# The first two modulation sections with the weights as the stationary operand, and one context load instead of two

## The chip, the cores and the metric

The kernel runs on one core of a Trainium2 chip. The metric is the device time of one execution in microseconds, and shorter is better. The core has four engines that matter here: TensorE (PE, matmuls; its loads of the stationary operand are listed as PEld), VectorE (DVE), ScalarE (ACT) and GpSimd (POOL). SyncE (SP) only issues DMAs; ACT issues some as well. TensorE's clock has two levels, 1.2 and 2.4 GHz; a granted clock of 0.50 is the lower one and 1.00 the upper one.

## The reference

The reference is a two-layer backbone for 256 context tokens and 256 latent tokens of width 1024. Before anything else of a layer is computed, two conditioning vectors become six shifts, scales and gates each:

```python
cond_lat = jax.nn.silu(c)          # (1, 1024)
cond_ctx = jax.nn.silu(c_ctx)      # (1024,)
for layer in range(DEPTH):
    l_sh1, l_sc1, l_g1, l_sh2, l_sc2, l_g2 = jnp.split((cond_lat @ mod_w[layer] + mod_b[layer])[:, None, :], 6, axis=-1)
    c_sh1, c_sc1, c_g1, c_sh2, c_sc2, c_g2 = jnp.split(cond_ctx @ mod_w[layer] + mod_b[layer], 6, axis=-1)
    hl = modulate(rmsnorm(x, norm_g[layer, 0]), l_sh1, l_sc1)
    hc = modulate(rmsnorm(ctx, norm_g[layer, 0]), c_sh1, c_sc1)
    ...
```

`modulate(h, shift, scale)` is `h * (1 + scale) + shift`. All is float32. Sections 0 and 1 (the first shift and the first scale) of layer 0 are a product of a 2 x 1024 matrix with a 1024 x 2048 one, 8.4 MB of weights. The projections, the retention and attention of layer 0, its FFN, layer 1 and the experts follow, and each needs what came before it.

## The kernel before, in words

The program is written once in straight line, and the framework makes from it the order of instructions on each engine. That order is not wholly the written one: the second load of the context, written behind the mixer of layer 0 in `between`, is issued 23.93 us after the start. Each engine then works through its own order strictly in turn, and waits on semaphores. DMAs share a small set of semaphores, so that a queue can also wait for an older transfer that used the same one.

At the start, `columns` loads small vectors as rows, turns them with a TensorE transpose and copies the result into SBUF, so that element p of chunk k stands on partition p of column k (lines 198 to 211). It is used for `cvec` (the two conditioning vectors) and for `vec` (norm gains and other vectors; `voff` remembers where each begins). `cond` (line 216) holds the silu of both vectors, with k in columns and the two vectors in the first two of 32 lanes. `Xl` is the latent stream. The context is loaded into `Xc` by `load_xc`, first into `xnp0`, the pool of the start, and later again into `xcp`, a pool that stays.

`layer0` (line 492) calls `mod(0)`, then `first_two(xnp0)` and then `norm_hT(xnp0, range(4), A1, B1)`. In `first_two`, sixteen tiles `mraw` of 128 x 1024 weights (512 KB each, twelve buffers) come over SP's queue (line 300). Each serves two matmuls (line 313) in which `cond` (128 x 32) is the stationary operand and 512 weight columns stream through; the four blocks of 512 columns go to four groups of 32 output partitions. The result is a row vector: bias is added (line 315), four transposes turn it into columns (line 318), and `put` writes `B1` (line 290) and `A1 = (1 + scale) * gain` (line 288).

`norm_stats` (lines 376 to 387) takes the row statistics of all four token blocks and scales them into `xn`. `norm_hT` transposes `xn` (line 400), applies `A1` and `B1` (line 405, `htmp`) and splits the result into `hTh` and `hTl` (lines 272 and 273). The first projection starts at once behind it: `proj_tok` loads weights into `raw` (line 253), splits them into `whi` and `wlo` (lines 262 and 263) and multiplies in three passes (lines 267 to 269). Later sections of the modulation (`section`, lines 335 and 337) are done on VectorE, among the projections and the mixer.

Of the kernel before, what the change touches and what calls it, by code (L numbers as in the profile page):

```python
# [8 lines left out]
F32 = mybir.dt.float32  # L9
# [4 lines left out]
ALU = mybir.AluOpType  # L14
# [93 lines left out]
def seq(*gens):  # L108
    for g in gens:
        yield from g  # L110
# [20 lines left out]
def _build(top, tc, nc, V, S, G, T, I, O):  # L131
    cp = top.enter_context(tc.tile_pool(name="const", bufs=1))
    st = top.enter_context(tc.tile_pool(name="st", bufs=4))
    cur = {}

    def open_right(key, name, bufs=1):
        cur[key] = ExitStack()
        return cur[key].enter_context(tc.tile_pool(name=name, bufs=bufs, side="right", reuse_waits="tile"))
# [19 lines left out]
    def bank(kind):  # L158
        def take(name=kind):
            turn[kind] = turn.get(kind, -1) + 1  # L160
            n = use[kind][turn[kind] % len(use[kind])]
            return ps.tile([128, 512], F32, name=name, tag=f"b{n}")
        return take
    acc, tpp, att, ybank = (bank(k) for k in ("acc", "tp", "at", "y"))
# [4 lines left out]
    def const_(shape, name, dt=F32):  # L169
        return cp.tile(shape, dt, name=name)  # L170
# [11 lines left out]
    ident = cc("ident")  # L182
# [6 lines left out]
    xcp = open_right("xe", "xc")  # L189
# [5 lines left out]
    n0 = ExitStack()  # L195
    xnp0 = n0.enter_context(tc.tile_pool(name="n0", bufs=1))

    def columns(name, parts):

        n = sum(p[2] for p in parts)  # L200
        rows = xnp0.tile([n, 128], F32, name=name + "_r")
        r0 = 0
        for nm, src, k in parts:
            nc.scalar.dma_start(rows[r0:r0 + k], src)
            voff[nm] = r0
            r0 += k
        out = const_([128, n], name)
        t0 = tpp()
        T.transpose(t0[:, 0:n], rows, ident[0:n, 0:n])
        V.tensor_copy(out, t0[:, 0:n])  # L210
        return out

    voff = {}
    cvec = columns("cvec", (("c", I["c"].rearrange("o (k p) -> (o k) p", p=128), 8),
                            ("cc", I["c_ctx"].rearrange("(k p) -> k p", p=128), 8)))
    cond = const_([128, 8, 32], "cond")
# [3 lines left out]
    def load_xc(pool, src):  # L220
        cur["Xc"] = pool.tile([128, 2, D], F32, name="Xc")
        nc.scalar.dma_start(cur["Xc"], src.rearrange("(b p) d -> p b d", p=128))

    nc.scalar.dma_start(Xl, I["x"][0].rearrange("(b p) d -> p b d", p=128))
    load_xc(xnp0, I["ctx"][0])
    vec = columns("vec", (
        ("ng", I["norm_g"].rearrange("l i (k p) -> (l i k) p", p=128), 64),
        ("mu", I["rwkv_mu"].rearrange("o (k p) -> (o k) p", p=128), 15),
# [9 lines left out]
    def bcast_rows(dst, src, q=nc.scalar):  # L238
        n = src.shape[-1]
        q.dma_start(dst, bass.AP(tensor=src.tensor, offset=src.offset, ap=[[0, 128], [1, n]]))  # L240
# [36 lines left out]
    def mod(layer):  # L277
        A1, B1, A2, B2 = (const_([128, 8, 2], n) for n in ("A1", "B1", "A2", "B2"))

        by_half = lambda dst: dst.rearrange("p (s b) r -> p b s r", s=2)  # L280

        def put(q, tv):

            if q == 1:
                o = voff["ng"] + layer * 32
                ng = vec[:, o:o + 8].rearrange("p (s b) -> p b s", s=2)
                for r in range(2):
                    V.scalar_tensor_tensor(by_half(A1)[:, :, :, r], tv[:, :, :, r], 1.0, ng, op0=ALU.add, op1=ALU.mult)
            else:
                V.tensor_copy(by_half({0: B1, 3: B2, 4: A2}[q]), tv[:, :, :, 0:2])  # L290

        def bias(row, c0):
            G.memset(row, 0.0)
            n = row.shape[0]
            for r in range(2):
                nc.scalar.dma_start(row[r:n:32], I["mod_b"][layer, c0:c0 + 16 * n].rearrange("(s n) -> s n", s=n // 32))

        def load(pool, bufs, k, c0):
            w = pool.tile([128, 1024], F32, name="mraw", tag="mraw", bufs=bufs)
            nc.sync.dma_start(w, I["mod_w"][layer, k * 128:(k + 1) * 128, c0:c0 + 1024])  # L300
            return w

        def first_two(pool):

            row = cur["m"].tile([128, 1024], F32, name="modrow2", tag="part0", bufs=1)[:, :512]
            bias(row, 0)
            a = acc()
            for k in range(8):
                for s2 in range(2):
                    w = load(pool, 12, k, s2 * 1024)  # L310
                    for sj in range(2):
                        s = 2 * s2 + sj
                        T.matmul(a[32 * s:32 * s + 32], cond[:, k, :], w[:, sj * 512:(sj + 1) * 512],
                                 start=(k == 0), stop=(k == 7), tile_position=(0, 32 * s))
            V.tensor_tensor(row, row, a, op=ALU.add)
            t = tpp()
            for b in range(4):
                T.transpose(t[:, b * 128:(b + 1) * 128], row[:, b * 128:(b + 1) * 128], ident)
            tv = t.rearrange("p (b q s j) -> p q b s j", b=4, q=2, s=2)
            put(0, tv[:, 0])  # L320
            put(1, tv[:, 1])

        def section(q):

            w_ = cur["m"]
            streams = 1 if layer and q > 1 else 2
            part = [w_.tile([128, 1024], F32, name=f"part{r}", tag=f"part{r}", bufs=1) for r in range(streams)]
            for k in range(8):  # L330
                w = load(w_, 2, k, q * 1024)
                for r in range(streams):
                    c_ = cond[:, k, r:r + 1]
                    if k == 0:
                        V.tensor_scalar(part[r], w, c_, None, op0=ALU.mult)
                    else:
                        V.scalar_tensor_tensor(part[r], w, c_, part[r], op0=ALU.mult, op1=ALU.add)  # L337
                if k == 4:
                    rn = cur["h"].tile([128, 1024], F32, name="modrow", tag="raw", bufs=cur["rb"])
                    row, ngr = rn[0:64, 0:512], rn[0:64, 512:1024]  # L340
                    bias(row, q * 1024)
                    if q in (2, 4, 5):
                        G.memset(ngr, 1.0)
                        for r in range(2):
                            nc.scalar.dma_start(ngr[r:64:32], I["norm_g"][layer, {2: 1, 4: 2, 5: 3}[q]]
                                                .rearrange("(s n) -> s n", s=2))
                    if q == 4:
                        G.tensor_scalar(row, row, 1.0, None, op0=ALU.add)
                yield
            a = tpp()  # L350
            for r in range(streams):
                for s in range(2):
                    T.matmul(a[32 * s:32 * s + 32], cur["pick"][:, r], part[r][:, s * 512:(s + 1) * 512],
                             start=(r == 0), stop=(r == streams - 1), tile_position=(0, 32 * s))
            V.tensor_tensor(row, row, a[0:64], op=ALU.add)
            if q in (2, 4, 5):
                V.tensor_tensor(row, row, ngr, op=ALU.mult)
            if q > 1:
                for r in range(2):
                    nc.scalar.dma_start(I["mrow"][layer, q // 2 - 1, r, q % 2 * 1024:q % 2 * 1024 + 1024]  # L360
                                        .rearrange("(s n) -> s n", s=2), row[r:64:32])
            if q not in (2, 5):
                t = tpp()
                for b in range(4):
                    T.transpose(t[:, b * 64:(b + 1) * 64], row[:, b * 128:(b + 1) * 128], ident[0:64, 0:64])
                put(q, t[:, 0:256].rearrange("p (b s j) -> p b s j", b=4, s=2))

        def rowb(pool, n, r, name, tag=None, q=nc.scalar):

            t = pool.tile([128, D], F32, name=name, tag=tag or name, bufs=1)  # L370
            bcast_rows(t, I["mrow"][layer, n // 2 - 1, r, n % 2 * 1024:n % 2 * 1024 + 1024], q)
            return t

        mods[layer] = (first_two, section, rowb, A1, B1, A2, B2)

    def norm_stats(xnp, blks):
# [115 lines left out]
    def layer0():  # L492
        mod(0)
        first_two, section, rowb, A1, B1, A2, B2 = mods[0]
# [20 lines left out]
        de, xx, u, z, w, lg = (st.tile([128, 8], F32, name=f"lg_{i}", bufs=1) for i in range(6))  # L515
# [32 lines left out]
        t = {}  # L548
# [100 lines left out]
        m = seq(*(section(n) for n in (2, 3, 4)))  # L649
# [13 lines left out]
        first = {}  # L663

        def between():
            load_xc(xcp, I["ctx"][0])
            for i in range(4):
                first[i // 2, i % 2] = wsplit(gu_load(i // 2, i % 2, 0, 2), pre, G)

# [34 lines left out]
    def gu_load(k4, x, f0, n):  # L704
        w = (I["ffn_w_gate"], I["ffn_w_up"])[x][0]
        return wload(w[k4 * 512:(k4 + 1) * 512, f0 * 128:(f0 + n) * 128].rearrange("(a p) f -> p a f", p=128), 4, n * 128)
# [1176 lines left out]
```

## Time and profile before

| what | value |
|---|---|
| time, three runs | 2129.33, 2130.3, 2136.47 us, median 2130.3 |
| the profiled execution | 2132.66 us, of which 2130.9 us is the span from the first to the last instruction |
| TensorE busy | 2038.5 us (96%), mean granted clock 0.973 |
| VectorE busy | 1646.4 us (77%) |
| ScalarE busy | 1210.4 us (57%) |
| DMA | 494 MB, mean 232 GB/s |

The busy share is an average over stages that have different limits. For a change in the first 40 us, only that stage and what waits for it matter, and the busy share of TensorE is no measure of how fast its matmuls run.

### The profile page before, as it was taken

The page shows a single profiled execution, that of the slowest core. Times are in us where ns is not written, and L with a number is a line of the kernel's source. Part 1 is how long each engine was busy: PE and PEld are TensorE (multiplying, and loading weights), DVE is VectorE, ACT ScalarE, POOL GpSimd, SP SyncE. Part 2 cuts the span into 40 slices and gives each one's busy share as a digit, 9 for nine tenths or more (in the row PEclk, how much of TensorE's full clock was granted, in tenths as well). Part 3 has the DMA queues.
Part 4 walks back from the last instruction along what each step waited for, and adds up shares of the span by engine and source line. Part 5 has one row for each costly group of instructions (what it writes and reads, how often), then busy time and mean ns, then how long its engine had stood idle before and what let it go on. Part 6 is the DMA issues. An engine that isn't in the chain of part 4 may idle for free. (4 is left out here: it accounts for less than half of the span.)

```text
span 2130.9 us, 30220 instructions
## 1 busy us (share of the span) xinstructions
PE 2038.5 (96%) x11649; PEld 1621.1 (76%) x11650; DVE 1646.4 (77%) x2083; ACT 1210.4 (57%) x1557; POOL 152.6 (7%) x211
## 2 busy tenths in 40 slices
PE   7999989999999899869989999999999999999997
PEld 2767778878788666758877888888788787888875
DVE  3967793675556657687579999889989899889987
ACT  3543343222234445632348777777777777777775
POOL 0211110000000110184010000000000000000000
PEclk9999999999999999977899999999999999999999
DMA  8535352466645331100197999999999999999993
GB/s 299 163 106 169 105 175 60 149 229 206 190 157 188 102 90 55 34 19 12 62 333 267 361 307 362 337 352 360 349 347 341 352 376 353 334 356 361 360 352 143
DMA packets 224203, 494.00 MB, mean 232 GB/s; under 512 B 11355, under 2 KB 45262, under 8 KB 224054
## 3 DMA queue, kind: packets, MB, share of 16 engines
q1 hardware_dynamic: 219968, 482.62, 65.0%
q10 hardware_dynamic: 4086, 9.40, 1.3%
q8 instruction: 93, 1.52, 0.3%
q14 instruction: 56, 0.46, 0.1%
HBM read 490.87 MB, written 1.11 MB: 231 GB/s over the span
## 5 line engine op out<-in xcount | busy, mean ns | idle before, releaser
L273 DVE TENSOR_TENSOR mlo<-mraw,mhi 128x1024 fp32r<-128x1024 f32 x668 | 789.0, 1220 | 79.4 <-ACT mhi L272 62.6
L272 ACT ACTIVATE mhi<-mraw 128x1024 fp32r<-128x1024 f32 x668 | 683.3, 1057 | 106.6 <-PE y L269 49.0
L262 ACT ACTIVATE whi<-raw 128x1024 fp32r<-128x1024 f32 (+1 forms) x150 | 152.9, 1023 | 276.3 <-PE acc L269 108.8
L263 DVE TENSOR_TENSOR wlo<-raw,whi 128x1024 fp32r<-128x1024 f32 (+1 forms) x146 | 172.7, 1186 | 136.0 <-ACT whi L262 135.5
L267 PE MATMUL acc<-hTh,whi 128*128 128x512 f32 (+1 forms) x504 | 190.6, 380 | 0.0
L268 PE MATMUL acc<-hTl,whi 128*128 128x512 f32 (+1 forms) x504 | 186.6, 371 | 0.0
L269 PE MATMUL acc<-hTh,wlo 128*128 128x512 f32 (+1 forms) x504 | 185.7, 369 | 0.0
L268 PE MATMUL g<-mlo,xh 128*128 128x512 f32 x448 | 182.4, 407 | 0.0
L337 DVE SCALAR_TENSOR_TENSOR part<-mraw,cond,part 128x1024 f32<-128x1024 f32 x112 | 149.8, 1358 | 41.9 <-DMA mraw<-in_mod_w 41.7
L267 PE MATMUL g<-mhi,xh 128*128 128x512 f32 x448 | 178.7, 399 | 0.0
L267 PE MATMUL u<-mhi,xh 128*128 128x512 f32 x448 | 177.4, 396 | 0.0
L268 PE MATMUL u<-mlo,xh 128*128 128x512 f32 x448 | 177.3, 396 | 0.0
L269 PE MATMUL u<-mhi,xl 128*128 128x512 f32 x448 | 177.1, 395 | 0.0
L269 PE MATMUL g<-mhi,xl 128*128 128x512 f32 x448 | 177.1, 395 | 0.0
L268 PE MATMUL y<-mlo,acts 128*128 128x512 f32 x448 | 175.8, 392 | 0.3 <-DVE mlo L273 0.3
L269 PE MATMUL y<-mhi,acts 128*128 128x512 f32 x448 | 174.8, 390 | 0.0
L267 PE MATMUL y<-mhi,acts 128*128 128x512 f32 x448 | 151.4, 390 | 0.0
L268 PE MATMUL acc<-wlo,hTh 128*128 128x512 f32 x336 | 135.1, 402 | 4.5 <-DVE wlo L263 4.5
L267 PE MATMUL acc<-whi,hTh 128*128 128x512 f32 x336 | 135.8, 407 | 3.4 <-ACT whi L262 2.0
L269 PE MATMUL acc<-whi,hTl 128*128 128x512 f32 x336 | 134.0, 400 | 0.0
L267 PEld LDWEIGHTS acc<-hTh,whi 128*128 128x128 f32 x504 | 95.4, 190 | 22.5 <-issue 4.1
L268 PEld LDWEIGHTS acc<-hTl,whi 128*128 128x128 f32 x504 | 95.0, 189 | 17.6 <-issue 2.8
(433 smaller groups left out, 3378.3 us busy)
## 6 DMA issues: line engine op xcount, KB each, us to landing
mraw<-in_moe_w_gate SPq DMA_DIRECT2D x112, 1024.0 KB
mraw<-in_moe_w_up SPq DMA_DIRECT2D x112, 1024.0 KB
mraw<-in_moe_w_down SPq DMA_DIRECT2D x110, 1024.0 KB
mraw<-in_mod_w SPq DMA_DIRECT2D x96, 512.0 KB
raw<-in_ffn_w_down SPq DMA_DIRECT2D x32, 512.0 KB
raw<-in_odd_w_in SPq DMA_DIRECT2D x26, 512.0 KB
raw<-in_even_w_in SPq DMA_DIRECT2D x24, 512.0 KB
raw<-in_ffn_w_gate SPq DMA_DIRECT2D x20, 512.0 KB
```

The costliest lines, as they stand in the source:

```text
L262: S.activation(h, v, AF.Copy)
L263: (eng or V).tensor_tensor(l, v, h, op=ALU.subtract)
L267: T.matmul(out, ah, bh, start=first, stop=False)
L268: T.matmul(out, ah, bl, start=False, stop=False)
L269: T.matmul(out, al, bh, start=False, stop=last)
L272: S.activation(hi, src, AF.Copy)
L273: eng.tensor_tensor(lo, src, hi, op=ALU.subtract)
L337: V.scalar_tensor_tensor(part[r], w, c_, part[r], op0=ALU.mult, op1=ALU.add)
```

## The change

The weights become the stationary operand. Each 128 x 1024 tile now serves eight matmuls of 128 x 128 weights, through which the two columns of `cond` stream; output j of a tile is a pair of columns, so that the result already stands in columns. All 16 output blocks lie in one PSUM bank, with one start and one stop. The bias `mb` comes through `columns` (16 rows of 128, one DMA, one transpose, one copy), into the pool of the start. Three VectorE instructions write `B1` and `A1`. The row of biases with its memset and two DMAs, the addition to it and the four transposes go. The context is loaded once, into the pool that stays.

```diff
-    def columns(name, parts):
+    def columns(name, parts, pool=None):
...
-        out = const_([128, n], name)
+        out = pool.tile([128, n], F32, name=name) if pool else const_([128, n], name)
...
-    load_xc(xnp0, I["ctx"][0])
+    load_xc(xcp, I["ctx"][0])
...
         def first_two(pool):
 
-            row = cur["m"].tile([128, 1024], F32, name="modrow2", tag="part0", bufs=1)[:, :512]
-            bias(row, 0)
+            mb = columns("mb", (("mb", I["mod_b"][layer, 0:2048].rearrange("(k p) -> k p", p=128), 16),), pool)
             a = acc()
+            v = a[:, 0:32].rearrange("p (k r) -> p k r", r=2)
             for k in range(8):
                 for s2 in range(2):
                     w = load(pool, 12, k, s2 * 1024)
-                    for sj in range(2):
-                        s = 2 * s2 + sj
-                        T.matmul(a[32 * s:32 * s + 32], cond[:, k, :], w[:, sj * 512:(sj + 1) * 512],
-                                 start=(k == 0), stop=(k == 7), tile_position=(0, 32 * s))
-            V.tensor_tensor(row, row, a, op=ALU.add)
-            t = tpp()
-            for b in range(4):
-                T.transpose(t[:, b * 128:(b + 1) * 128], row[:, b * 128:(b + 1) * 128], ident)
-            tv = t.rearrange("p (b q s j) -> p q b s j", b=4, q=2, s=2)
-            put(0, tv[:, 0])
-            put(1, tv[:, 1])
+                    for j in range(8):
+                        T.matmul(v[:, 8 * s2 + j], w[:, j * 128:(j + 1) * 128], cond[:, k, 0:2],
+                                 start=(k == 0 and s2 == 0 and j == 0), stop=(k == 7 and s2 == 1 and j == 7),
+                                 skip_group_check=True)
+            cols = lambda x, i: x[:, i:i + 8][:, :, None].to_broadcast([128, 8, 2])
+            V.tensor_tensor(B1, v[:, 0:8], cols(mb, 0), op=ALU.add)
+            V.tensor_tensor(A1, v[:, 8:16], cols(mb, 8), op=ALU.add)
+            V.scalar_tensor_tensor(A1, A1, 1.0, cols(vec, voff["ng"] + layer * 32), op0=ALU.add, op1=ALU.mult)
...
         def between():
-            load_xc(xcp, I["ctx"][0])
             for i in range(4):
```

## Rows read from the trace of the kernel before

**Rows 1.** The page's head and its busy time by engine.
```profile
span 2130.9 us, 30220 instructions
PE 2038.5 (96%) x11649; PEld 1621.1 (76%) x11650; DVE 1646.4 (77%) x2083; ACT 1210.4 (57%) x1557; POOL 152.6 (7%) x211
```

**Rows 2.** Timeline of the start: start us, length us, engine, line, what.
```profile
6.89 1.94 PE L313 MATMUL acc<-mraw,cond 128*32 128x512 f32 x8 [0.53 <-ACT cond L218]
...
11.76 1.92 PE L313 MATMUL acc<-mraw,cond 128*32 128x512 f32 x4 [0.79 <-DMA mraw<-in_mod_w]
...
17.15 0.25 ACTq L204 DMA_DIRECT2D vec_r<-in_rwkv_r_k  x1
...
20.54 0.42 PE L209 MATMUL tp<-cst_all,vec_r 99*128 99x99 f32 x1
...
23.93 0.39 ACTq L222 DMA_DIRECT2D Xc<-in_ctx  x1
...
32.13 1.12 PE L400 MATMUL tp<-cst_all,xn 128*128 128x128 f32 x4
...
37.80 1.05 PE L313 MATMUL acc<-mraw,cond 128*32 128x512 f32 x4 [0.23 <-DMA mraw<-in_mod_w]
38.96 0.69 DVE L315 TENSOR_TENSOR modrow<-modrow,acc 128x512 f32<-128x512 f32 x1 [8.96 <-PE acc L313]
...
39.70 0.66 PE L318 MATMUL tp<-cst_all,modrow 128*128 128x128 f32 x4 [0.84 <-DVE modrow L315]
40.40 0.17 DVE L290 COPY B<-tp 128x16 f32<-128x16 f32 x1 [0.75 <-PE tp L318]
40.49 0.23 DVE L288 SCALAR_TENSOR_TENSOR A<-tp,vec 128x8 f32<-128x8 f32 x2
40.76 1.90 DVE L405 TENSOR_SCALAR htmp<-tp,A,B 128x256 f32<-128x256 f32 x4
```

**Rows 3.** Waits of the first 60 us: total us, times, longest.
```profile
PEld acc L313 <- DMA mraw<-in_mod_w: 24.2, 14, 3.9
```

**Rows 4.** Durations of line 313 at the start: ns min/median/max.
```profile
L313 PE MATMUL acc<-mraw,cond x64: 592/1061/1063, 6.9 to 38.3; 128*32 128x512 f32 x64
```

**Rows 5.** Stretches at the start: busy us (count) by engine, granted clock, DMA share, GB/s.
```profile
6.90:23.00 16.10, 13.27 (x33) 1.50 (x33) 0.26 (x1) 3.58 (x7) 0.00 (x0) 1.00 0.91 332
...
26.50:33.30 6.80, 6.00 (x18) 1.41 (x20) 3.19 (x13) 1.71 (x4) 0.00 (x0) 0.50 1.02 416
33.30:38.90 5.60, 4.13 (x16) 0.49 (x16) 0.00 (x0) 0.00 (x0) 0.00 (x0) 1.00 1.03 396
```

**Rows 6.** Timelines of matmuls with eight streamed columns, at 945, 1087 and 1100 us.
```profile
945.08 3.58 PE L1091 MATMUL tp<-cst_rwkv,rkT 128*128 128x8 f32 x16 [2.62 <-DVE rkT L1086]
...
945.07 3.49 PEld L1091 LDWEIGHTS tp<-cst_rwkv,rkT 128*128 128x128 f32 x16 [2.75 <-DVE rkT L1086]
...
1099.86 1.92 PE L1541 MATMUL lg<-rt,xT 128*128 128x8 f32 x16 [1.30 <-ACT xT L1531]
```

**Rows 7.** Durations of those lines: ns min/median/max, first and last start.
```profile
L1091 PE MATMUL tp<-cst_rwkv,rkT x16: 361/361/383, 945.1 to 948.3; 128*128 128x8 f32 x16
...
L1541 PE MATMUL lg<-rt,xT x32: 247/256/277, 1099.9 to 1107.1; 128*128 128x8 f32 x32
```

**Rows 8.** Stretches with small matmuls in layer 1.
```profile
945.00:948.30 3.30, 3.23 (x16) 3.23 (x16) 2.93 (x10) 0.00 (x0) 2.93 (x5) 0.50 0.00 0
944.70:985.60 40.90, 40.52 (x460) 35.03 (x462) 25.15 (x69) 10.49 (x19) 27.98 (x69) 0.50 0.07 21
```

**Rows 9.** Stretches behind the start.
```profile
42.50:50.00 7.50, 7.21 (x36) 5.71 (x37) 7.50 (x14) 3.60 (x5) 0.00 (x0) 1.00 0.52 164
...
40.00:60.00 20.00, 18.88 (x96) 14.99 (x95) 19.25 (x34) 8.95 (x13) 0.00 (x0) 1.00 0.58 182
60.00:80.00 20.00, 18.93 (x85) 15.24 (x84) 17.72 (x32) 14.94 (x31) 0.00 (x0) 1.00 0.62 218
80.00:120.00 40.00, 37.36 (x171) 28.32 (x170) 38.14 (x75) 21.28 (x45) 13.82 (x15) 1.00 0.43 133
120.00:160.00 40.00, 37.99 (x168) 25.98 (x167) 25.88 (x51) 16.95 (x36) 5.21 (x6) 1.00 0.29 92
```

**Rows 10.** DMA issues by line, KB each.
```profile
Xc<-in_ctx ACTq DMA_DIRECT2D x2, 1024.0 KB
```

## The prediction

> **What bounds the kernel now.** I read the page first. TensorE is busy for 2038.5 of 2130.9 us [rows 1], but that is an average; the change touches the first 40 us and one load, so the question is what ends that stage, and whether what follows passes a shift on.
>
> The timeline of the start and the waits answer the first half [rows 2, 3]. The matmuls of line 313 come in bursts, each when a weight tile has landed, and TensorE's weight loads stand 24.2 us in all for those tiles. The last burst begins at 37.80. From 26.5 to 38.9 us the DMA engines are full, at 396 to 416 GB/s [rows 5]. So the stage is bound by DMA, and TensorE has room: a tile costs it one pair of passes, 1.92 us at the lower level and 1.05 at the upper one [rows 2], and 16 tiles take 32 us to come. Behind the last burst stand an addition, four transposes and the writes of B1 and A1; `htmp`, the first user, starts at 40.76.
>
> The reader should look at the clock as well. The granted clock reads 1.00 for the first 23 us [rows 5], but one matmul of line 313 takes 1061 ns there and 592 at best [rows 4]. A factor near two is the step between the two levels, so I take the start to be at 1.2 GHz whatever the column says. It reads 0.50 from 26.5 to 33.3, and 1.00 only behind a stretch in which matmuls with 512 columns had followed one another.
>
> Does a shift pass through? From 42.5 to 50 us TensorE is busy for 7.21 of 7.50 us and VectorE for all of it; from 40 to 160 us TensorE idles 1.12 + 1.07 + 2.64 + 2.01 = 6.8 us of 120 [rows 9]. Each later stage needs the one before it. I pass the shift on in full, but for what these 6.8 us can give.
>
> **The change, part by part.**
>
> *Matmuls.* Each tile now serves eight matmuls with 128 x 128 weights instead of two with 128 x 32, so there are 16 x 8 = 128 where there were 32. A float32 matmul is recorded as two passes, each with its own weight load: the 32 old ones are 64 records [rows 4], and the router's line 1541 is 16 matmuls in the code and 32 records [rows 7]. So the new ones are 256 passes, each with a load of 128 columns and two streamed columns. The trace has no stream of two columns; the nearest is eight with the same weights. At the lower level, 16 of them take 3.58 us, the last one 0.36, so one follows another in (3.58 - 0.36) / 15 = 0.215 us; at the upper level it is (1.92 - 0.26) / 15 = 0.111 [rows 6, 7]. Does it get cheaper with two columns? The transposes of line 400 stream 128 columns with as large a weight load, and four take 1.12 us at the lower level [rows 2], that is 0.23 each ((1.12 - 0.42) / 3, taking the 0.42 of the vec transpose for the last). From 128 columns to eight hardly anything changes, and the weight loads fill 3.23 of 3.30 us [rows 8]: the price is the weight load, not the columns. So 256 passes are 256 x 0.215 = 55.0 us at the lower level, and 256 x 0.111 = 28.4 at the upper one, with 3.44 and 1.78 us for a tile. The tiles land every 2 us on average (32 us for 16), so TensorE becomes the bound at the lower level.
>
> The Trainium skill (TensorE: Matmul & The Clock Gate, LDWEIGHTS) gives the load of a stationary operand as its column count over 1.2 GHz, whatever the clock; by that, as an estimate from the page, a pass would take 0.107 us and all of them 27.3 instead of 55.0. The rows at the lower level show twice that, so here the measurement decides.
>
> *Which level?* This is the choice on which the forecast rests. The stretch from 944.7 to 985.6 us holds small matmuls and 128-column transposes with hardly a pause: TensorE is busy for 40.52 of 40.90 us, its weight loads for 35.03, and the granted clock is 0.50 throughout [rows 8]. It begins with the very stream of line 1091 that I price with. The new stream starts at the lower level and streams still fewer columns. I take the lower level to its end.
>
> *The rest on TensorE's queue.* The transpose for vec (0.42), one for mb (0.42 at most, the same instruction with fewer columns) and the four of line 400 (1.12) stand among the passes: 1.9 us [rows 2]. The transposes for vec and mb wait for small DMAs on ACT's queue. vec's last one is issued at 17.15, and its transpose runs at 20.54; mb's comes right behind. Everything behind such a transpose on TensorE waits too. If four tiles stand ahead of it (6.89 + 4 x 3.44 = 20.7), it costs nothing; if only one does, some 10 us. I take 1.
>
> *Removed behind the last pass.* From the last burst's end (37.80 + 1.05 = 38.85) to 40.76 there are 1.9 us [rows 2]. In their place stand three small VectorE instructions. Lines 290 and 288 take 0.17 and 0.23 for such sizes; with a start delay like the 0.11 us between 38.85 and 38.96, I take 0.8 in all.
>
> *The shift.* 6.89 + 55.0 + 1.9 + 1.0 + 0.8 = 65.6 us where it was 40.76: `htmp` starts 24.8 us later.
>
> *What follows.* TensorE reaches the projection at the lower level, where before it was at the upper one. The stretch at 0.50 in the start was 6.8 us long [rows 5]; at half pace as much again costs 3.4 us at most if the work is TensorE's alone, and nothing if VectorE holds it up anyway. I take 2. Against it, the first weight tiles of the projection are long there and can be split while VectorE and ScalarE wait, and steps of the next modulation section may be pulled forward; that is worth between 0 and the 6.8 us of idle time. I take 2. The two cancel.
>
> *The context load.* One of two loads of 1024 KB goes [rows 10], issued at 23.93 [rows 2], in the middle of the weight tiles. At 410 GB/s it holds the DMA engines for 2.6 us. With TensorE as the bound that cover makes it worth nothing; with DMA as the bound it would be worth all 2.6. The bias row's memset and two DMAs stood beside waits for weights; nothing follows from their going. The twelve weight buffers are now released every 3.44 us, the first at 10.3; four tiles must wait for one, the last until 6.89 + 4 x 3.44 = 20.7, well ahead of its use. SP's queue behind them holds the projection's weights, which are then there before 65 us.
>
> *Sum.* 24.8 + 2 - 2 = 24.8 us on the profiled execution's 2132.66, which makes 2157.5. That execution is 2.4 us above the median of the runs, so I forecast 2155.
>
> **The rivals.**
>
> *The clock rises early (not slower).* If weight loads one after another, or the transposes among them, lift the clock, then after some 6.8 us at half pace (3.4 us lost) the passes cost 28.4. 6.89 + 28.4 + 3.4 + 1.4 + 0.8 = 40.9, with 1.4 for the other transposes at up to full pace, and a stall for vec of 0 to 5 us, since four tiles are then done by 17. That is 0 to +5 us: about 2133 on the median's scale. It decides as soon as the lift comes before about half of the tiles. For it: line 1541 runs its 16 passes in 1.92 us at the upper level [rows 6]. Against it: the 41 us of [rows 8]. The Trainium skill (TensorE: Matmul & The Clock Gate, Why this matters for your kernels) says that a TensorE kept continuously busy gets its full clock. By that rule this rival is the forecast; the 40.52 us busy at 0.50 contradict it for small matmuls, which is why its chance is low.
>
> *TensorE keeps up with DMA (faster).* If the upper level were there from the start, the last tile, earlier by 2.6 us, lands near 35.2; with 1.8 and 0.8 behind it, `htmp` starts at 37.8, 3 us early: 2127. More than 0.3% needs nearly all of the 6.8 us of idle time too. The level at the start speaks against it.
>
> *The clock rises midway.* With half of the tiles at each level the passes take 41.7 us, the shift is about 11.5, the time 2142.
>
> *vec's or mb's transpose stands early in TensorE's order.* Behind one tile, it costs 9 us more than I took: 2164. In the kernel before, it stands behind seven tiles, but their passes were cheaper.
>
> **How the numbers follow.** Chances: forecast 0.70, early transpose 0.08, midway 0.07, clock rises early 0.12, TensorE keeps up 0.03. The forecast's own bounds: no stall (-1), no loss at the restart (-2) and all idle time regained (-5) give 2147; a microsecond more of stall, the full 3.4 for the restart and nothing regained give 2159. The early transpose reaches to 2168. With the upper part of the midway case I put the range at 2143 to 2168; it leaves out the 0.15 of the two cases at the old time and part of the midway one. Within 0.3% means within 6.4 us, about what a measurement here tells from no change: faster 0.03, same 0.12, slower 0.85.
>
> **What would show it.** The new line's records: 256 loads and 256 passes, a median pass near 360 ns, one behind another every 0.215 us, and hardly any wait for `mraw` after the second tile. The last pass ends near 64 us, `htmp` starts near 65.6, and from 40 to 64 us DMA is nearly idle, which it was not. One load of Xc. Behind that, each stage's start is about 25 us later than before. I am wrong if the passes' median is near 256 ns, if TensorE still waits for weight tiles, or if the stages at 330 us and later have a shift that differs from that of `htmp` by more than 7 us.

## The result

The changed kernel takes 2155.68 us (median of six runs, 2150.77 to 2158.8), the kernel before 2132.28 (six runs, 2129.33 to 2136.47). The ratio is 1.0107, with a 95% interval of 1.009 to 1.0123: 23 us slower, clear of the 0.3% that a measurement can tell. The forecast was 2155, with 2143 to 2168 as its range. It lands closer than its working: the median of the kernel before, over six runs, is 2 us above the 2130.3 of the three runs that it started from, and the shift is 23.4 us and not 24.8.

The profiled execution of the changed kernel has a span of 2153.4 us, 22.5 more than that of before [rows 1]. These are its page's head and its busy time by engine:

```profile
span 2153.4 us, 30595 instructions
PE 2070.8 (96%) x11838; PEld 1674.4 (78%) x11839; DVE 1647.1 (76%) x2083; ACT 1211.8 (56%) x1557; POOL 152.3 (7%) x210
```

TensorE's busy share is the same 96%, so it says nothing of the loss. What says it is the timeline of the start (start us, length us, engine, line, what), which answers to [rows 2]:

```profile
6.98 24.05 PE L312 MATMUL acc<-cond,mraw 128*128 128x2 f32 x112 [0.53 <-ACT cond L218]
...
30.89 0.41 PE L209 MATMUL tp<-cst_all,vec_r 99*128 99x99 f32 x1
31.09 3.46 PE L312 MATMUL acc<-cond,mraw 128*128 128x2 f32 x16
34.48 0.28 PE L209 MATMUL tp<-cst_all,mb_r 16*128 16x16 f32 x1
...
50.01 13.65 PE L312 MATMUL acc<-cond,mraw 128*128 128x2 f32 x64
63.70 0.17 DVE L316 TENSOR_TENSOR B<-acc,mb 128x16 f32<-128x16 f32 x1 [23.60 <-PE acc L312]
63.79 0.17 DVE L317 TENSOR_TENSOR A<-acc,mb 128x16 f32<-128x16 f32 x1
63.99 0.17 DVE L318 SCALAR_TENSOR_TENSOR A<-A,vec 128x16 f32<-128x16 f32 x1
64.20 1.90 DVE L402 TENSOR_SCALAR htmp<-tp,A,B 128x256 f32<-128x256 f32 x4
```

The reader should see three things. The first row holds 112 passes without a wait for `mraw`, where the old line 313 stood between tiles [rows 3]. The vec transpose stands behind seven tiles, long after its data are there, and costs no wait of TensorE. VectorE waits 23.6 us for the last pass, and `htmp` starts at 64.20, which is 23.4 us later than before.

The durations of the new line (ns min/median/max, first and last start) stand against [rows 4]:

```profile
L312 PEld LDWEIGHTS acc<-cond,mraw x256: 288/333/370, 7.0 to 63.2; 128*128 128x128 f32 x128
L312 PE MATMUL acc<-cond,mraw x256: 213/352/374, 7.0 to 63.3; 128*128 128x2 f32 x128
```

In stretches of the start and behind it (busy us and count for PE, PEld, DVE, ACT and POOL, then granted clock, DMA share, GB/s), compare [rows 5 and 9]:

```profile
26.50:33.30 6.80, 6.80 (x34) 6.80 (x34) 0.26 (x1) 0.00 (x0) 0.00 (x0) 1.00 1.03 414
...
40.00:64.00 24.00, 23.66 (x112) 23.57 (x112) 0.36 (x4) 0.00 (x0) 0.00 (x0) 1.00 0.00 1
```

From 40 to 64 us DMA, VectorE, ScalarE and GpSimd do next to nothing, and TensorE's weight loads fill 23.57 of the 24 us. The clock column reads 1.00 here, as it did at the start of the kernel before; the passes' 352 ns are those of the lower level. A run below, in which the level changes early, shows the same passes beside 0.50.

Later stages, by the first and last start of their lines, answer to [rows 7] (line 1091 is 1087 here, 1541 is 1537):

```profile
L1087 PE MATMUL tp<-cst_rwkv,rkT x16: 361/361/379, 968.3 to 971.5; 128*128 128x8 f32 x16
...
L1537 PE MATMUL lg<-rt,xT x32: 247/256/378, 1123.0 to 1130.4; 128*128 128x8 f32 x32
```

They stand 23.2 and 23.1 us later than before (968.3 against 945.1, and 1123.0 against 1099.9): almost the whole shift of the start arrives there.

### The profile page after: what moved, and what is told of

It is laid out like the page before. It is cut to its first block, busy times and chain, and to the rows that moved or that the text cites. A ratio compares the mean times of both kernels' runs of the same rounds, so it can differ in the third digit from the quotient of the medians.

```text
span 2153.4 us, 30595 instructions
## 1 busy us (share of the span) xinstructions
PE 2070.8 (96%) x11838; PEld 1674.4 (78%) x11839; DVE 1647.1 (76%) x2083; ACT 1211.8 (56%) x1557; POOL 152.3 (7%) x210
## 5 line engine op out<-in xcount | busy, mean ns | idle before, releaser
L267 PEld LDWEIGHTS acc<-hTh,whi 128*128 128x128 f32 x504 | 95.9, 191 | 22.5 <-issue 4.1
```

Source lines behind the costliest of these rows:

```text
L267: T.matmul(out, ah, bh, start=first, stop=False)
```

## The experiments

The times of the first four are compared with the kernel before on one chip (median 2133.45 us, 23 runs), those of the last four with one run of it (2134.74).

**One load, old matmuls.** The kernel before, with the context part of the change alone.

```diff
-    load_xc(xnp0, I["ctx"][0])
+    load_xc(xcp, I["ctx"][0])
...
         def between():
-            load_xc(xcp, I["ctx"][0])
```

> The kernel before with only the context load changed: loaded once, at the start, into the pool that stays. My theory (DMA bounds the start of the kernel before, and 1 MB fewer among the weight tiles is worth up to 2.6 us there): the last burst of line 313 starts 1 to 2.6 us earlier than 37.80, htmp near 38.5 to 40, and the time is 0 to 3 us below that of the kernel before, within what a measurement can tell. Rival (the load change contributes to the loss, through another order on the queues or another layout of the pool): 3 us or more above the kernel before.

Measured: 2129.93 us (12 runs), ratio 0.9988, interval 0.9978 to 0.9999. This ratio and the next ones are those that the measurement gave; they are not the quotients of the medians given here (0.9983 in this case). The timeline of that run:

```profile
34.14 1.05 PE L313 MATMUL acc<-mraw,cond 128*32 128x512 f32 x4 [0.22 <-DMA mraw<-in_mod_w]
35.30 0.69 DVE L315 TENSOR_TENSOR modrow<-modrow,acc 128x512 f32<-128x512 f32 x1 [5.26 <-PE acc L313]
36.04 0.65 PE L318 MATMUL tp<-cst_all,modrow 128*128 128x128 f32 x4 [0.85 <-DVE modrow L315]
36.73 0.17 DVE L290 COPY B<-tp 128x16 f32<-128x16 f32 x1 [0.75 <-PE tp L318]
36.82 0.23 DVE L288 SCALAR_TENSOR_TENSOR A<-tp,vec 128x8 f32<-128x8 f32 x2
```

The last burst starts 3.66 us earlier, and still waits for its tile: DMA bounds the old form, and this half of the change is a gain of 3.7 us at the start, 1.1 more than the 2.6 us that one megabyte takes. That is ahead of what was expected (1 to 2.6 us, and `htmp` near 38.5 to 40; it starts at 37.09). It is the only version here whose interval lies below 1, by 0.12%, and it barely leaves out 1.

**New matmuls, two loads.** The changed kernel, with the context loaded as before: the diff above the other way round.

> The changed kernel with the context loaded twice again: the matmul part of the change alone. My theory (TensorE's weight loads bound the start): the same start as in the changed kernel, htmp near 64 us and the time 21 to 26 us above the kernel before; the extra megabyte is hidden. Rival (the single load matters as much as the matmuls): a time that differs from that of the changed kernel by 3 us or more.

Measured: 2156.26 us (4 runs), ratio 1.0115, interval 1.0099 to 1.0131; the changed kernel's is 1.0107. In this run's timeline:

```profile
50.40 13.65 PE L312 MATMUL acc<-cond,mraw 128*128 128x2 f32 x64
...
64.59 1.90 DVE L402 TENSOR_SCALAR htmp<-tp,A,B 128x256 f32<-128x256 f32 x4
```

`htmp` starts at 64.59 instead of 64.20. The matmuls alone make the loss, and the second megabyte is hidden behind them but for 0.4 us. The same edit is worth 3.7 us in one form and 0.4 in the other, since another engine sets the end.

**Half of the passes.** Every second matmul is left out, so that half of each sum is missing.

```diff
                     for j in range(8):
+                        if (j + k) % 2:
+                            continue
                         T.matmul(v[:, 8 * s2 + j], w[:, j * 128:(j + 1) * 128], cond[:, k, 0:2],
```

> The changed kernel with every second of the 128 matmuls left out (for each output block four of the eight products are summed, so half of the sum is missing); all sixteen weight tiles are loaded and used. 128 passes where there were 256. My theory (0.215 us a pass at the lower level, and TensorE the bound): 27.5 us less of passes, so TensorE would be done near 36.5; but the tiles then bound the stage again, the last one landing at 33 to 36 with 8 passes behind it; htmp starts at 37 to 41 and the time is within 3 us of the kernel before. Rival (the loss is not in the passes but in the form: waits, order, PSUM, a cold restart behind them): at least 8 us above the kernel before.

Measured: 2129.58 us (10 runs), ratio 0.9992, interval 0.9981 to 1.0002. The durations of its matmuls, who waited, and the timeline:

```profile
L314 PE MATMUL acc<-cond,mraw x128: 212/352/375, 7.5 to 40.5; 128*128 128x2 f32 x128
...
PEld acc L314 <- DMA mraw<-in_mod_w: 3.8, 3, 2.5
...
34.05 6.83 PE L314 MATMUL acc<-cond,mraw 128*128 128x2 f32 x32
...
41.41 1.90 DVE L404 TENSOR_SCALAR htmp<-tp,A,B 128x256 f32<-128x256 f32 x4
...
L334 DVE TENSOR_SCALAR part<-mraw,cond x16: 739/742/1027, 62.1 to 582.2; 128x1024 f32<-128x1024 f32 x16
```

A pass is as long as before, TensorE waits for tiles again, and the loss is gone from the times (by the medians the run is 3.9 us below the kernel before, by the ratio 1.7; within 3 was expected). `htmp` starts 0.4 us behind the range given: the last 32 passes still run one behind another, so TensorE and DMA bound this stage by turns. The form itself and its order cost nothing that can be measured in the time; the number of passes does. The restart behind it is not free: `htmp` is 0.65 us later than in the kernel before, but line 334, the first modulation step (line 335 before), starts at 62.1 instead of 58.9, so 2.5 us more are lost there. In the time of the whole kernel they can't be seen.

**Twice the passes.** Each matmul is issued twice, so that the sums are twice too large.

```diff
-                    for j in range(8):
+                    for j in range(16):
+                        j, again = j // 2, j % 2
                         T.matmul(v[:, 8 * s2 + j], w[:, j * 128:(j + 1) * 128], cond[:, k, 0:2],
-                                 start=(k == 0 and s2 == 0 and j == 0), stop=(k == 7 and s2 == 1 and j == 7),
-                                 skip_group_check=True)
+                                 start=(k == 0 and s2 == 0 and j == 0 and again == 0),
+                                 stop=(k == 7 and s2 == 1 and j == 7 and again == 1), skip_group_check=True)
```

> The changed kernel with each matmul of the first two sections issued twice in a row, so that the sums are twice too large: 512 passes. My theory: 256 x 0.215 = 55 us more in the start, htmp near 119, and as much in the time (50 to 57 us above the changed kernel), with the clock at the lower level all the way. Rival (a longer stream lifts the clock, or a weight load of the same block costs less the second time): 25 to 40 us more.

Measured: 2207.56 us (one run), 52 above the changed kernel. Its durations and the start of `htmp`:

```profile
L313 PE MATMUL acc<-cond,mraw x512: 212/352/374, 7.6 to 118.6; 128*128 128x2 f32 x171
...
119.48 1.90 DVE L403 TENSOR_SCALAR htmp<-tp,A,B 128x256 f32<-128x256 f32 x4
```

256 passes more move `htmp` by 55.28 us, 0.216 each, and 111 us of such a stream don't bring the upper level: the median pass still takes 352 ns.

**A wider stream.** All 32 lanes of `cond` stream, 30 of them zeros.

```diff
-            v = a[:, 0:32].rearrange("p (k r) -> p k r", r=2)
+            v = a.rearrange("p (k r) -> p k r", r=32)
...
-                        T.matmul(v[:, 8 * s2 + j], w[:, j * 128:(j + 1) * 128], cond[:, k, 0:2],
+                        T.matmul(v[:, 8 * s2 + j], w[:, j * 128:(j + 1) * 128], cond[:, k],
...
```

> The changed kernel with all 32 lanes of the conditioning tile streamed through each weight block instead of two (30 of them zeros, their results unused): as many weight loads, 16 times the columns. My theory (the weight load sets the price of a pass, and a stream of such short matmuls does not lift the clock): passes still 0.215 us apart, htmp at 63 to 66 us, the time within 4 us of the changed kernel. Rival (how many columns stream decides the clock, and 32 are enough): the passes are 0.11 us apart before long, htmp at 41 to 50 us, the time 14 to 23 us below the changed kernel.

Measured: 2151.18 us (one run), 4.5 below the median of the changed kernel (within 4 was expected), and inside the range of its six runs. Durations and timeline:

```profile
L312 PE MATMUL acc<-cond,mraw x256: 261/401/422, 6.9 to 63.3; 128*128 128x32 f32 x128
...
64.23 1.90 DVE L402 TENSOR_SCALAR htmp<-tp,A,B 128x256 f32<-128x256 f32 x4
```

Sixteen times the columns move `htmp` by 0.03 us. A pass is recorded as longer, 401 ns against 352, but the passes stand no further apart. So the price of a pass is not its columns, as forecast from eight columns and from 128. That it is the weight load is argued from the loads' records, which fill the time; no run here has a narrower weight block.

**A warm start.** Seven idle matmuls of 512 columns ahead of the first weight block, while TensorE would wait for it.

```diff
+            z = pool.tile([128, 512], F32, name="zero")
+            V.memset(z, 0.0)
+            spin = ps.tile([128, 512], F32, name="spin", tag="b5")
+
+            def warm(n):
+                for _ in range(n):
+                    T.matmul(spin, z[:, 0:128], z, start=True, stop=True)
...
+            warm(7)
             for k in range(8):
```

> The changed kernel with seven idle matmuls of 512 columns (zeros, result unused) ahead of the first weight block, while TensorE waits for the first weights. My theory (a stream of weight loads with two columns neither lifts the clock nor keeps it): if the level rises at all, it falls back, most passes stay at 361 ns, and htmp starts at 57 to 66 us. Rival (the stream keeps the level that it starts with): median pass near 256 ns, htmp at 37 to 44 us, the time 20 to 25 us below the changed kernel.

Measured: 2156.67 us (one run). The timeline, stretches of this run, and the durations of the passes that start between 49.7 and 59.9 us:

```profile
9.04 3.53 PE L312 MATMUL spin<-zero 128*128 128x512 f32 x7
12.41 20.08 PE L320 MATMUL acc<-cond,mraw 128*128 128x2 f32 x112
...
65.66 1.90 DVE L410 TENSOR_SCALAR htmp<-tp,A,B 128x256 f32<-128x256 f32 x4
...
10.00:20.00 10.00, 10.00 (x62) 8.56 (x60) 0.00 (x0) 2.55 (x5) 0.00 (x0) 0.83 0.96 359
20.00:30.00 10.00, 10.00 (x48) 10.00 (x49) 0.00 (x0) 3.00 (x5) 0.00 (x0) 0.50 0.92 339
...
50.00:60.00 10.00, 10.00 (x49) 10.00 (x48) 0.00 (x0) 0.00 (x0) 0.00 (x0) 0.50 0.00 0
...
L320 PE MATMUL acc<-cond,mraw x43: 212/352/352, 49.7 to 59.9; 128*128 128x2 f32 x43
```

The first 112 passes take 20.08 us instead of 24.05, so some ran at the upper level, and the stretch from 10 to 20 us has a mean of 0.83. Then the clock falls and stays at 0.50, with TensorE busy all the time. Here the column reads what the pass durations say, 352 ns at 0.50. The 4.0 us that were gained are lost again, as the stream begins 5.4 us later than in the changed kernel, behind the idle matmuls: `htmp` comes at 65.66 instead of 64.20.

**Idle matmuls in between.** As above, and two or four of them behind each weight tile.

```diff
                                  skip_group_check=True)
+                    warm(2)        # second run: warm(4)
```

> As the run with the warm start, and two idle matmuls of 512 columns behind each weight tile's eight matmuls. They cost 32 x 0.43 = 14 us at the upper level and 27 at the lower one (a 512-column matmul's two passes at the rate of the old line 313). If the columns streamed in between hold the clock up: passes 0.11 us apart, 28 + 14 us in all, htmp near 52 to 55, the time 9 to 13 us below the changed kernel. If they don't: 55 + 27 us, htmp near 92, the time some 28 us above it. My theory (the level is the matter, and wide matmuls hold it) expects the first, without being sure that two are enough.

> As before with four idle matmuls behind each weight tile: 64 x 0.43 = 27 us at the upper level, 55 at the lower. My theory: the level stays up for most of it, the passes are 0.11 us apart, 28 + 27 us in all, htmp at 64 to 70 us, so that twice the work on TensorE takes as long as the changed kernel's. Rival (the price of a pass does not hang on the level): passes 0.215 us apart with the level up, htmp at 90 or more.

Measured: 2210.72 us with two, 2184.97 with four (one run each). Timelines, one stretch of each, and the durations of the passes from about 60 us on, two first:

```profile
22.27 3.41 PE L320 MATMUL acc<-cond,mraw 128*128 128x2 f32 x16
25.55 3.76 PE L312 MATMUL spin<-zero 128*128 128x512 f32 x4
...
60.00:70.00 10.00, 10.00 (x26) 6.38 (x27) 0.00 (x0) 0.00 (x0) 0.00 (x0) 0.50 0.01 2
...
L320 PE MATMUL acc<-cond,mraw x130: 212/352/353, 59.8 to 114.6; 128*128 128x2 f32 x130
...
119.47 1.90 DVE L411 TENSOR_SCALAR htmp<-tp,A,B 128x256 f32<-128x256 f32 x4 [4.01 <-PE tp L406]
```

and four:

```profile
28.76 1.84 PE L320 MATMUL acc<-cond,mraw 128*128 128x2 f32 x16
30.47 3.68 PE L312 MATMUL spin<-zero 128*128 128x512 f32 x8
...
60.00:70.00 10.00, 10.00 (x48) 6.42 (x47) 7.28 (x7) 0.00 (x0) 0.00 (x0) 1.00 0.57 176
...
L320 PE MATMUL acc<-cond,mraw x112: 167/251/251, 60.1 to 93.0; 128*128 128x2 f32 x112
...
97.26 1.90 DVE L411 TENSOR_SCALAR htmp<-tp,A,B 128x256 f32<-128x256 f32 x4 [3.51 <-PE tp L406]
```

With four the clock stays up, and a tile's 16 passes take 30.47 - 28.76 = 1.71 us, 0.107 a pass; with two it falls, and they take 25.55 - 22.27 = 3.28, 0.205 a pass. (The first pass of such a group starts early, so both are a little below the spacings of 0.111 and 0.215 that were forecast.) The loads and the columns are the same, and the median pass takes 251 ns beside 1.00 and 352 beside 0.50. So the level makes the factor of two in a pass, and the theory stands. The price of the idle matmuls was wrong in my expectation, by a factor of two at either level: eight passes take 28.76 - 25.25 = 3.51 us at the upper one, where the row

```profile
25.25 3.68 PE L312 MATMUL spin<-zero 128*128 128x512 f32 x8
```

begins, that is 0.88 for a matmul and not 0.43. I had taken it from the old line 313, whose matmuls run two at a time on different groups of output partitions (in the trace of before, the two of a tile start within 10 ns of each other). So `htmp` of the run with four was expected at 64 to 70 us and came at 97.26, with the right level: in the rival's range of 90 or more, but not with the rival's passes of 0.215 us. The one with two missed its first case, since the level fell, and its second (92 us, at 119.47), by the price. Neither is a way to use the new form.

## Why the prediction was right

*The bound now.* DMA bounds the old start: the last burst of the run with one load came 3.66 us earlier and still waited for its tile.

*Price of the passes.* 256 passes were forecast, and there are 256. The spacing is (24.05 - 0.35) / 111 = 0.2135 us in the first row of the changed kernel's timeline, taking 0.35 for the last; 0.215 was forecast. From the first pass to the end of the last (6.98 to 63.66) there are 56.7 us, where the passes, the other transposes and the stall were put at 57.9. The run with twice the passes gives the same price (0.216), the one with half of them takes the loss away, and the one with 32 columns shows that the columns are not the price. That the weight load is, and not another fixed cost of a pass that goes with the clock, is not shown by a run of its own.

*The level.* It stayed at 1.2 GHz to the end. The passes at 352 ns say so for the changed kernel; the warm start shows 352 ns beside a granted clock of 0.50. The rival that a busy TensorE gets its clock back is refuted for this stream: neither 57 us nor 111 us of it brought the upper level, and the warm start lost it. The Trainium skill (TensorE: Matmul & The Clock Gate, Why this matters for your kernels) gives the rule behind that rival, to keep TensorE continuously busy for its full clock. The traces agree with it for the run with four idle matmuls behind each tile (251 ns beside 1.00), and not for the stream alone or with two (352 ns, TensorE busy for all of the 10 us from 60 to 70 at 0.50).

*The rest of TensorE's queue.* I took 1.9 us for the other transposes and 1.0 for a stall. There was no stall, eight transposes of line 397 stood among the passes instead of four, and three VectorE instructions took 0.54 us from the last pass (63.66) to `htmp`, where I had 0.8. `htmp` came at 64.20, not 65.6.

*What follows.* The restart at the lower level was forecast as 2 us. The first matmul of the projection comes 2.78 us behind `htmp` (66.98) and not 1.71 as before (42.47). With four idle matmuls, where the level was up, it is 1.71 again (98.97). These are the rows of the changed kernel, of the one before, and of the run with four:

```profile
66.98 1.63 PE L267 MATMUL acc<-whi,hTh 128*128 128x512 f32 x3
...
42.47 0.74 PE L267 MATMUL acc<-whi,hTh 128*128 128x512 f32 x2
...
98.97 0.49 PE L267 MATMUL acc<-whi,hTh 128*128 128x512 f32 x1
```

It is 1.71 with one load too, and 2.78 or 2.79 with two loads, half of the passes, twice the passes and the warm start; with 32 columns it is 1.88, at the lower level, with another order of the first transposes. Line 332, the first modulation step on VectorE behind it (335 before), is 25.8 us late (84.7 in the changed kernel, 58.9 before), 2.4 more than `htmp`:

```profile
L332 DVE TENSOR_SCALAR part<-mraw,cond x16: 737/744/1036, 84.7 to 603.7; 128x1024 f32<-128x1024 f32 x16
...
L335 DVE TENSOR_SCALAR part<-mraw,cond x16: 736/740/754, 58.9 to 578.6; 128x1024 f32<-128x1024 f32 x16
```

That is about the term as forecast. The 2 us that I set against it were right only in sum, and at the wrong place, so here the forecast was lucky. I expected them within the first 160 us, from weight tiles split early and work pulled forward. Nothing of it came: from 40 to 64 us ScalarE does nothing and VectorE 0.36 us, and at the last start of this line, 603.7 against 578.6, the shift is still 25.1. It is 23.1 at the router, and 22.5 in the span. One step on the way can be read. At 895 us of the kernel before the shift is still 24.5 (line 1011), at 920 it is 23.5 (line 972). Between them the granted clock stands at 0.50 for 6.8 us before and for 3.4 in the changed kernel, as these stretches of 9 us show, before first:

```profile
899.00:908.00 9.00, 6.96 (x143) 6.48 (x143) 3.99 (x8) 2.51 (x6) 1.37 (x5) 0.62 0.10 33
...
923.40:932.40 9.00, 6.85 (x134) 6.26 (x126) 4.84 (x9) 3.06 (x6) 2.27 (x7) 0.81 0.11 33
```

The other traces go the same way: in the five that have 3.4 us there, too, the shift against before falls by 0.5 to 2.2 us between these two lines, and in the three that have 6.8 it moves by -0.1 to 1.0. Whether this belongs to the change or to the one execution that was profiled stays open, as does the rest of the 2.6 us: the kernel before spreads by 9 us over 23 runs (2128.13 to 2137.22).

*The context load.* Forecast as worth nothing in the new form and up to 2.6 us with DMA as the bound; measured 0.4 and 3.7 at `htmp`. Where the 1.1 us beyond the megabyte's own time come from stays open.

## What to carry to other kernels

Here the thin operand was better kept stationary: turning the two round replaced 64 passes with 32 weight columns each by 256 with 128, and such a pass has the same price with 2 columns behind it as with 32. Before a stage is given more TensorE work because TensorE waits there, compare the new work of one tile with the time between two tiles, and do it at the clock level which that stage really has, read from durations of the same engine at the same place. At the upper level a tile's passes took 1.71 us in the run with four idle matmuls, less than the 2 us between two tiles; at the lower level, where this stage is, they take 3.4. When a change has two parts, time each alone: here the smaller one was a small gain that the larger one hid.

## What the runs showed that was not expected

The granted clock reads 1.00 from the start until the first change of level in a trace, whatever the level is: 352 ns passes stand beside 1.00 in the changed kernel, and the same passes beside 0.50 in the warm start. Durations decide there.

In the warm start the upper level did not survive the stream: 112 passes began at 12.41 us, the granted clock averages 0.83 from 10 to 20 us and is 0.50 from 20 us on, with TensorE busy without a pause. A float32 matmul of 512 columns with a weight block of 128 x 128 takes 0.88 us at the upper level in the run with four idle matmuls, about twice what a reading of two at a time on separate groups of output partitions had suggested.
